# A two-block transformer kernel: score products over all 128 rows, two pools of banks for the gates, the input scaled inside its transposing product

## The chip, the core and the metric

One NeuronCore of a Trainium2 chip runs the whole program in one launch. The metric is device time in microseconds (us). TensorE (PE) has two rows in the profile: PE are the matrix products, PEld the loads of the stationary operand, which can run beside a product. VectorE is DVE, ScalarE is ACT, GpSimd is POOL, and SP issues DMA transfers. L163 is line 163 of the kernel before.

## The reference, cut to what matters

`x` is [1, 512, 1024] in float32, and everything is float32. The first block mixes tokens by a banded attention and an RWKV-7 recurrence, merges the two under gates and ends in a feed-forward net. The second block has two layers: mLSTM beside forgetting attention, then a state-space mixer beside pooling, each followed by a convolved gated feed-forward net. The parts that the change touches:

```python
# first block: 8 heads of 64, scores scaled by 1/8, relative bias
h = rms_norm(x, pre_mix_g); proj = h @ w_in
logits = einsum(q, k) * HEAD_A**-0.5 + rel_bias ; p = softmax(logits) ; y_a = p @ v
y_b = rwkv7_time_mix(...)      # has the bonus (r * r_k * k').sum(-1) * v
merged = gate_a * (y_a @ proj_a) + gate_b * (y_b @ proj_b)
# second block, layer 0: 8 heads of 64, causal, with forget gates
logits = einsum('bhqd,bhkd->bhqk', qb, k) * scale + fq[..., :, None] - F[..., None, :]
```

## The kernel before, in words

The dense products dominate. Each float32 operand is split into a high and a low part of the tensor engine's reduced format, and a product is the sum of three (high-high, low-high, high-low). `dense_A` (L144 to L173, products on L163) gives feature tiles of W^T x for 512 tokens, two banks of PSUM a call; `dense_B` (L259, products on L281) gives token tiles. Weight chunks come by SP's queue into a ring of two and are split by ACT (L132) and DVE (L133).

Everything is unrolled. The framework's scheduler fixes each engine's order of instructions at build time: it goes by program order, takes what its own cost estimate finds ready, and so fills gaps of the attention and of the recurrences with dense products. At run time each engine takes its list strictly in that order and waits on semaphores. `order(a, b)` (L222) gives the scheduler an order of issue between two instructions and no data dependence.

The places that matter here:

- **Start** (`block1_in`, L466 to L507). For each of four token tiles ACT sums the squares of x (L491), DVE scales (L375), POOL takes the power -1/2 (L376), DVE multiplies the tile [128, 1024] by the result in place (L496), and PE transposes eight blocks of it into eight banks (L498). ACT and DVE then split the banks into xT (L502, L503), and the first dense product may begin. POOL's list has, behind the four powers, the transfers of `par` and `cst` (L495), the clear of a zero tile (L556), three clears of the state tiles S (L1440) and four transfers of zeros (L559), which have an `order` edge from L554 on DVE.
- **RWKV operands** (`rwkv_half`, twice, each for f = 0 and 1). DVE makes k' in the tile `ta` (L1323, L1324), POOL multiplies `ta` into the tile KB (L1325), DVE overwrites `ta` with the bonus operand (L1327), and PE sums it over heads (L1329).
- **Attention** (`attention_heads`, called by `attention1`, L1519, and by `layer0`, L801; twice four heads each time). A unit is one head and one of four query tiles t. PE makes the scores (L1569) of 128 queries and 128(t+1) keys; in layer 0 a bfloat16 product (L1571) adds the causal mask to the same bank. DVE adds the bias and takes the minimum of the negated row (L1573), ACT takes the exponential (L1575), PE transposes (L1583), ACT and DVE in turn copy (L1586, L1588), PE multiplies with v (L1597). Two heads share a tile of q and of k, one in rows 0 to 63 and one in rows 64 to 127, and the score product takes those 64 rows alone:

```python
hs = slice((h % 2) * 64, (h % 2) * 64 + 64)
nc.tensor.matmul(ps[:, 0:n], q[hs, t * 128 : t * 128 + 128], k[hs, 0:n], ...)
```

- **mLSTM** (`mlstm`, L944) has score products of the same kind over all 128 rows (L965). In `layer0` the four query tiles of the mLSTM and the query tiles of the attention come from one ring of four buffers (tag "q").
- **Gates** (`gate_mul`, L597). Each call is a `dense_A` of two banks from the pool `mm`, which has two; DVE multiplies each bank into the gate (L600), which frees it. There are four calls with `proj_a` and four with `proj_b`. The pools `ax` and `ax2` (two banks each) serve the RWKV half through `axt` (L1233), in turn. Behind the last call a new pool of eight banks opens for the product with `w_out`.

Of the kernel before, what the change touches and what calls it, by code (L numbers as in the profile page):

```python
# [26 lines left out]
# ---- per-feature vectors, features on partitions: name -> number of 128-columns  # L27
# [61 lines left out]
class Halves:  # L89
    """a tile [128, 2, 8, 256] (token half, feature tile, token) as [128 features, 512 tokens] of one feature tile"""  # L90
# [12 lines left out]
class Builder:  # L103
# [18 lines left out]
    # ---------------------------------------------------------------- weights  # L122
    def wchunk(self, src, a, b, keep=None):
        """a weight chunk of up to 1024 columns, split; keep: (pool, bufs) to hold it in"""
# [19 lines left out]
    def dense_A(self, xk, w, col0, pp, tag="mm", nf=2, half=None, ps=None, chunks=None, low=None):  # L144
        """nf feature tiles of W^T x, features on partitions; xk: [(hi, lo)] of [128, 512].
        half: only these 256 tokens (0 before 1, into the same banks); low: only the products with the weights'
        high (False, first) or low (True) parts"""
# [27 lines left out]
    def ahead(self, specs, pool):  # L175
        """the weights of begin, their low parts still to be made: (raw, hi, lo), the first two chunks
        in the ring of all weights; specs: (A or B, w, col0, columns)"""
# [18 lines left out]
    def ahead_hook(self, specs):  # L196
        """loads the next phase's first weights, when called"""
        def hook():
            self.nx_es.append(ExitStack())
            self.nx = self.ahead(specs, self.pool(self.nx_es[-1], "early", side="right"))  # L200
        return hook
# [22 lines left out]
    def begin(self, xk, specs):  # L224
        """the first products of a phase, the first half of the tokens before the last two tiles are there, from the
        weights loaded ahead; specs as there"""
# [32 lines left out]
    def dense_B(self, xk, w, col0, pp, tag="mm", width=512, toks=(0, 1, 2, 3), ps=None, chunks=None, low=None):  # L259
        """x W[:, col0:col0+width], tokens on partitions: {token tile: [128, width] PSUM view}; low: as in dense_A"""  # L260
# [26 lines left out]
    def close_B(self, xk, w, pp, add, post, T, pool, rest=None, lag=1, hook=None):  # L287
        """x W in two halves of the columns, the second token by token, so that what follows a token starts early;
        T: the transposes of a token, lag tokens late, the last ones in the next phase;
        rest: the tiles still to be added to the first half of the columns"""  # L290
# [16 lines left out]
    def mix_part(self, xk, w, pp):  # L307
        """column half 0: xN = ALPHA * xN + the part of the mixer's output that is ready"""
# [6 lines left out]
    def split(self, src, hi, lo, lo_eng=None):  # L315
        """hi + lo == src exactly; both of the tensor engine's reduced format"""
        nc = self.nc
        nc.scalar.activation(hi, src, AF.Copy)  # L318
        return (lo_eng or nc.vector).tensor_tensor(lo, src, hi.bitcast(F32), op=ALU.subtract)  # L319
# [17 lines left out]
    def to_T(self, xn, n, pair, t, pp, tag, k0=0):  # L337
        """xn: [128 tokens, n*128] -> columns t of pair's tiles k0..k0+n, split"""
# [20 lines left out]
    # ------------------------------------------------------------ row vectors  # L359
# [12 lines left out]
    def rsqrt(self, out, src, n, scale, eps):  # L372
        """out = (scale * src + eps) ** -0.5 on [128, n] columns"""
# [21 lines left out]
    def ln_apply(self, x, st, g, b):  # L395
        """layer norm over 1024 features in place, eps 1e-5; st: bn_stats of the halves"""
# [19 lines left out]
    # ------------------------------------------------------------------ setup  # L416
# [48 lines left out]
    # ---------------------------------------------------------- block 1 mixer  # L465
    def block1_in(self, pool):  # L466
# [3 lines left out]
        with ExitStack() as es:  # L470
# [13 lines left out]
            # the tensor engine's clock rises only while it works  # L484
# [4 lines left out]
            for t in range(4):  # L489
                r = self.stat(1)  # L490
                nc.scalar.activation(junk, xs[t], AF.Square, accum_out=r)  # L491
                i = self.rsqrt(r, r, 1, 1.0 / D, 1e-6)
# [3 lines left out]
                nc.vector.tensor_scalar(xs[t], xs[t], r, None, op0=ALU.mult)  # L496
                for k in range(8):
                    nc.tensor.transpose(ps[k][:, t * 128 : t * 128 + 128], xs[t][:, k * 128 : k * 128 + 128], self.ident)  # L498
# [10 lines left out]
    def block1_mix(self, es, stop, early_es, ch):  # L509
# [46 lines left out]
        nc.gpsimd.memset(z, 0.0)  # L556
# [40 lines left out]
    def gate_mul(self, y, w, fp, gts):  # L597
        ps = self.dense_A(self.klist(y), self.A[w], fp * 256, self.mm)
# [118 lines left out]
    # ------------------------------------------------- second block: shared  # L717
    def close_ln(self, xk, w, gn, bn, np_, pp, last=False, rest=None, hook=None):
        """xN = LN(xN + x w), then xT or the output; rest: xN's second half is still to be multiplied by ALPHA"""
# [73 lines left out]
    def log1pexp_neg_abs(self, out, u):  # L793
        """out = ln(1 + exp(-|u|))"""
# [5 lines left out]
    # ---------------------------------------------------------------- layer 0  # L800
    def layer0(self):  # L801
# [3 lines left out]
        with ExitStack() as es:  # L805
            with ExitStack() as es2:
# [9 lines left out]
                # the first two heads' v, and gates: forget rows 0:4 (mLSTM), 32:36 and 64:68 (attention), input rows 96:100  # L816
# [19 lines left out]
                # mLSTM inputs  # L836
# [38 lines left out]
                # columns by token: c (0:4 of each 64), exp(-m) (32:36)  # L875
# [35 lines left out]
                bf = self.brow(lp, "b_fv", 512)  # L911
                for hf in range(2):
                    fq = featT(2056, "q", hf, 0.125, lambda f: bq[:, 4 + f : 5 + f])
# [5 lines left out]
                    for t in range(4):  # L919
# [3 lines left out]
                        (fq[hh // 2], fk[hh // 2], hh, lambda j, hh=hh, fv=fv: fv[:, j, hh * 64 : hh * 64 + 64], os_[hh // 2],  # L923
# [12 lines left out]
    def rows_to_T(self, o, hi, lo):  # L936
        """o: [128 tokens, 4 token tiles, 128 features] -> [128 features, 512 tokens], split"""
# [6 lines left out]
    def mlstm(self, lp, q, k, mv, og, M, sel, col, y):  # L944
        """the matrix memory, quadratic form; returns the last head's transposes"""
# [734 lines left out]
```

## Time and profile before

| what | value |
|---|---|
| three timed runs | 2109.14, 2109.42 (median), 2111.05 us |
| profiled execution, its span | 2106.5 us |
| timed median less that span | 2.9 us |
| PE busy | 2065.2 us, 98% of the span |
| DVE, ACT, POOL busy | 53%, 36%, 8% |
| chain that ended last | PE 53%, every other engine and DMA 1% or less |

The page gives the profiled execution by its span; the 2.9 us are what lies around the span, with the scatter of the runs in it. To read the profile: PE is busy nearly all the time, so a microsecond is won or lost where PE's own work gets longer or shorter or where PE waits. Spacing, from the start of one product to the start of the next, is what a product costs in a stream; the duration of one overlaps the next one's.

### The profile page before, as it was taken

What the parts mean: (1) busy time and instruction counts of PE and PEld (TensorE: products, weight loads), DVE (VectorE), ACT (ScalarE), POOL (GpSimd) and SP (SyncE); (2) the same over time, 40 slices, a digit from 0 to 9 for tenths busy, and PEclk for the clock granted to TensorE, in tenths of its full rate; (3) what the DMA queues carried; (4) which work ended last, traced back from release to release, by engine and by line L of the source; (5) the groups of instructions that cost most, each with busy time, mean ns of one, the idle gap of its engine ahead of it and who ended that gap; (6) DMA issues with size and microseconds to landing.
All of it is one profiled execution on the core that took longest, in us unless ns stands there. A gap on an engine that the chain in (4) does not pass through costs nothing.

```text
span 2106.5 us, 27707 instructions
## 1 busy us (share of the span) xinstructions
PE 2065.2 (98%) x11216; PEld 1696.1 (81%) x11216; DVE 1114.8 (53%) x1831; ACT 765.6 (36%) x1213; POOL 163.5 (8%) x258
## 2 busy tenths in 40 slices
PE   8999999999999999999999999999999999999998
PEld 6678677777888888888777888888897789888886
DVE  4554455565532424544534765435576676543565
ACT  4431552144333423333333344314334534432441
POOL 1101110110000000112200000000020310000000
PEclk9999999999999999999999999999999999999999
DMA  6241125143233334232212322333322033332332
GB/s 205 71 88 42 31 71 107 42 145 104 77 94 100 93 97 125 76 107 80 61 60 91 101 89 91 100 106 109 112 74 80 31 110 101 100 100 90 100 100 91
DMA packets 175120, 192.52 MB, mean 91 GB/s; under 512 B 31560, under 2 KB 144712, under 8 KB 174992
## 3 DMA queue, kind: packets, MB, share of 16 engines
q1 hardware_dynamic: 169920, 173.40, 27.4%
q0 software_dynamic: 5072, 17.35, 2.6%
q8 instruction: 88, 1.44, 0.3%
q14 instruction: 40, 0.33, 0.1%
HBM read 184.94 MB, written 5.78 MB: 91 GB/s over the span
## 4 chain that ended last, share of the span: by engine, by line
PE 53%; DVE 1%; DMA 1%; POOL 1%; ACT 0%; issue 0%; DVEq 0%; ACTq 0%; POOLq 0%
PE psA L163 29%; PE psB L281 19%; PE pss L1569 1%; PE pso L1597 1%; PE pho L1137 1%; DMA raw<-od_w_out 1%; PE psT L345 0%; PE pspt L1583 0%; PE ppg L1176 0%; PE pss L1571 0%; PE pqk L965 0%; PE pho L973 0%; DVE wlo L133 0%; PE psr L941 0%; ACT whi L132 0%
## 5 line engine op out<-in xcount | busy, mean ns | idle before, releaser
L133 DVE TENSOR_TENSOR wlo<-raw,whi 128x1024 fp32r<-128x1024 f32 (+1 forms) x295 | 360.3, 1224 | 506.9 <-ACT whi L132 303.3
L132 ACT ACTIVATE whi<-raw 128x1024 fp32r<-128x1024 f32 (+1 forms) x295 | 311.7, 1056 | 635.7 <-PE psA L163 288.4
L163 PE MATMUL psA<-xTh,whi 128*128 128x512 f32 (+1 forms) x1616 | 416.9, 378 | 3.6 <-ACT xTh L318 1.7
L163 PE MATMUL psA<-xTl,whi 128*128 128x512 f32 (+1 forms) x1616 | 415.8, 377 | 1.3 <-DVE st L375 1.3
L163 PE MATMUL psA<-xTh,wlo 128*128 128x512 f32 (+1 forms) x1616 | 412.1, 376 | 0.0
L163 PEld LDWEIGHTS psA<-xTh,whi 128*128 128x128 f32 x1616 | 288.8, 189 | 59.6 <-issue 3.0
L163 PEld LDWEIGHTS psA<-xTl,whi 128*128 128x128 f32 x1616 | 291.1, 190 | 56.2 <-issue 2.7
L163 PEld LDWEIGHTS psA<-xTh,wlo 128*128 128x128 f32 x1616 | 286.9, 188 | 53.3 <-issue 2.3
L772 DVE SCALAR_TENSOR_TENSOR v<-psA,par,v 128x511 f32<-128x511 f32 (+1 forms) x176 | 131.3, 747 | 78.9 <-ACT v L770 76.5
L376 POOL TENSOR_TENSOR st<-st,mhalf 128x1 f32<-128x1 f32 (+1 forms) x40 | 32.9, 822 | 1266.7 <-DVE st L375 1266.5
L281 PE MATMUL psB<-whi,hidh 128*128 128x512 f32 x480 | 126.7, 390 | 0.0
L281 PE MATMUL psB<-wlo,hidh 128*128 128x512 f32 x480 | 126.4, 389 | 0.0
L281 PE MATMUL psB<-whi,hidl 128*128 128x512 f32 x480 | 126.4, 389 | 0.0
L281 PEld LDWEIGHTS psB<-whi,hidl 128*128 128x128 f32 x480 | 90.1, 188 | 18.8
L281 PEld LDWEIGHTS psB<-wlo,hidh 128*128 128x128 f32 x480 | 90.1, 188 | 18.7
L281 PEld LDWEIGHTS psB<-whi,hidh 128*128 128x128 f32 x480 | 90.0, 188 | 18.7
L770 ACT ACTIVATE v<-psA,par 128x512 f32<-128x512 f32 x88 | 67.8, 771 | 98.0 <-PE psA L163 98.0
L281 PE MATMUL psB<-whi,xTh 128*128 128x256 f32 (+2 forms) x320 | 53.4, 289 | 0.0
L281 PE MATMUL psB<-whi,xTl 128*128 128x256 f32 (+2 forms) x320 | 52.6, 287 | 0.6 <-DVE xTl L319 0.6
L318 ACT ACTIVATE xTh<-psT 128x512 fp32r<-128x512 f32 x40 | 21.9, 595 | 84.2 <-PE psT L345 84.2
L281 PE MATMUL psB<-wlo,xTh 128*128 128x256 f32 (+2 forms) x320 | 49.3, 286 | 0.0
L1575 ACT ACTIVATE sb<-sb,sm 128x128 f32<-128x128 f32 (+1 forms) x64 | 35.7, 559 | 34.1 <-DVE sm L1573 33.5
(406 smaller groups left out, 2503.2 us busy)
## 6 DMA issues: line engine op xcount, KB each, us to landing
raw<-fup SPq DMA_DIRECT2D x88, 512.0 KB, 3.5
raw<-fdn SPq DMA_DIRECT2D x44, 512.0 KB, 3.3
raw<-w_in SPq DMA_DIRECT2D x42, 512.0 KB, 3.8
raw<-w_up SPq DMA_DIRECT2D x32, 512.0 KB, 3.8
raw<-w_down SPq DMA_DIRECT2D x32, 512.0 KB, 3.7
raw<-ev_w_in SPq DMA_DIRECT2D x26, 512.0 KB, 3.7
raw<-od_w_in SPq DMA_DIRECT2D x14, 512.0 KB, 3.8
raw<-w_out SPq DMA_DIRECT2D x8, 512.0 KB, 3.7
```

The lines of the kernel that those rows point to most:

```text
L132: i = nc.scalar.activation(hi, raw, AF.Copy)
L133: self.w_ins = (i, nc.vector.tensor_tensor(lo, raw, hi.bitcast(F32), op=ALU.subtract))
L163: i = nc.tensor.matmul(o.rearrange("p (h t) -> p h t", h=2) if len(x.shape) == 3 else o, wt[:, k, fs], x, start=first and half != 1, stop= ...
L281: nc.tensor.matmul(ps[t], xk[k0 + k][a][:, t * 128 : t * 128 + 128], wt[:, k, :], start=first, stop=(end and k == kn - 1 and wt is lo), sk ...
L318: nc.scalar.activation(hi, src, AF.Copy)
L376: return nc.gpsimd.tensor_tensor(out, out, self.mhalf[:, 0:n], op=ALU.pow)
L770: nc.scalar.activation(v, ps[f], AF.Identity, scale=self.p(f"fcw{l}", 88 + ft), bias=self.p(f"fcb{l}", ft))
L772: nc.vector.scalar_tensor_tensor(v[:, sh:], ps[f][:, : 512 - sh], self.p(f"fcw{l}", tap * 44 + ft), v[:, sh:], op0=ALU.mult, op1=ALU.add)
L1137: nc.tensor.matmul(po[:, t, :], w[:, (t - j) * 128 : (t - j) * 128 + 128], xdt[j][:, h * 64 : h * 64 + 64], start=(j == 0 and t == 0), sto ...
L1569: nc.tensor.matmul(ps[:, 0:n], q[hs, t * 128 : t * 128 + 128], k[hs, 0:n], start=True, stop=cmask is None, skip_group_check=True)
L1575: nc.scalar.activation(sb[:, 0:n], sb[:, 0:n], AF.Exp, scale=-1.0, bias=sm[:, t : t + 1], accum_out=sm[:, 4 + t : 5 + t])
L1597: nc.tensor.matmul(po[:, t, :], pT[:, j * 128 : j * 128 + 128], v(j), start=(t == 0 and j == 0), stop=(j == t), skip_group_check=True)
```

## The change

- x is no longer multiplied in place. DVE makes a 128x128 diagonal tile from the identity and the factor, and the product that transposes multiplies by it (a float32 product in place of a transpose).
- The transfers of `par` and `cst` get their `order` edge from that diagonal of the last tile; the clears of the zero tile and of S get one from `x_ready`, the last instruction of L503 on DVE.
- The bonus operand goes into the tile `kkn`, whose readers are done, in place of `ta`.
- Every second call of `gate_mul` takes its two banks from `ax` and `ax2`.
- Each head has its own tile of q, 128 rows, of which the 64 rows of the other head are cleared once by POOL; the score product takes all 128 rows of q and k. In `attention1` these are four tiles beside the ring of k, in `layer0` the four buffers of the ring "q", for both halves. ACT writes the even heads' rows, DVE the odd heads'.
- Comments are removed; they change no instruction.

```diff
 block1_in:
-                i = self.rsqrt(r, r, 1, 1.0 / D, 1e-6)
+                self.rsqrt(r, r, 1, 1.0 / D, 1e-6)
+                dg = ld.tile([128, 128], F32, name=self.nm("dg"))
+                i = nc.vector.tensor_scalar(dg, self.ident, r, None, op0=ALU.mult)
                 if t == 3:
                     for n in ("par", "cst"):
                         self.order(i, nc.gpsimd.dma_start(getattr(self, n), A[n]))
-                nc.vector.tensor_scalar(xs[t], xs[t], r, None, op0=ALU.mult)
                 for k in range(8):
-                    nc.tensor.transpose(ps[k][:, t * 128 : t * 128 + 128], xs[t][:, k * 128 : k * 128 + 128], self.ident)
+                    nc.tensor.matmul(ps[k][:, t * 128 : t * 128 + 128], xs[t][:, k * 128 : k * 128 + 128], dg, start=True, stop=True)
 block1_mix:
-        nc.gpsimd.memset(z, 0.0)
+        self.order(self.x_ready, nc.gpsimd.memset(z, 0.0))
 gate_mul:
-        ps = self.dense_A(self.klist(y), self.A[w], fp * 256, self.mm)
+        ps = [self.axt(1, self.nm("psA")) for _ in range(2)] if fp % 2 else None
+        ps = self.dense_A(self.klist(y), self.A[w], fp * 256, self.mm, ps=ps)
 layer0:
+                fq = self.head_tiles(lp, 4, tag="q", bufs=4)
                 for hf in range(2):
-                    fq = featT(2056, "q", hf, 0.125, lambda f: bq[:, 4 + f : 5 + f])
+                    ps = self.dense_A(xk, W, 2056 + hf * 256, mm)
+                    for f in range(2):
+                        b = bq[:, 4 + 2 * hf + f : 5 + 2 * hf + f]
+                        nc.scalar.activation(fq[2 * f][0:64, :], ps[f][0:64, :], AF.Identity, scale=0.125, bias=b[0:64, :])
+                        nc.vector.tensor_scalar(fq[2 * f + 1][64:128, :], ps[f][64:128, :], 0.125, b[64:128, :], op0=ALU.mult, op1=ALU.add)
...
-                        (fq[hh // 2], fk[hh // 2], hh, lambda j, hh=hh, fv=fv: ...
+                        (fq[hh], fk[hh // 2], hh, lambda j, hh=hh, fv=fv: ...
 rwkv_half:
-            nc.vector.scalar_tensor_tensor(ta, r, self.p("r_k", ft), ta, op0=ALU.mult, op1=ALU.mult)
+            nc.vector.scalar_tensor_tensor(kkn, r, self.p("r_k", ft), ta, op0=ALU.mult, op1=ALU.mult)
...
-            nc.tensor.matmul(psb, self.c("bones", 128), ta, start=True, stop=True)
+            nc.tensor.matmul(psb, self.c("bones", 128), kkn, start=True, stop=True)
...
-            nc.gpsimd.memset(s, 0.0)
+            self.order(self.x_ready, nc.gpsimd.memset(s, 0.0))
 attention1:
+        qz = self.head_tiles(ap, 4)
         for hf in range(2):
...
+            ps = self.dense_A(xk, w_in, hf * 256, mm)
+            for f in range(2):
+                nc.scalar.activation(qz[2 * f][0:64, :], ps[f][0:64, :], AF.Copy, scale=0.125)
+                nc.vector.tensor_scalar(qz[2 * f + 1][64:128, :], ps[f][64:128, :], 0.125, None, op0=ALU.mult)
...
+    def head_tiles(self, pool, n, **kw):
+        out = [pool.tile([128, 512], F32, name=self.nm("qz"), **kw) for _ in range(n)]
+        for h, t in enumerate(out):
+            self.nc.gpsimd.memset(t[64:128, :] if h % 2 == 0 else t[0:64, :], 0.0)
+        return out
 attention_heads:
-            nc.tensor.matmul(ps[:, 0:n], q[hs, t * 128 : t * 128 + 128], k[hs, 0:n], start=True, stop=cmask is None, skip_group_check=True)
+            nc.tensor.matmul(ps[:, 0:n], q[:, t * 128 : t * 128 + 128], k[:, 0:n], start=True, stop=cmask is None, skip_group_check=True)
```

## Rows read from the trace of the kernel before

**Rows 1.** The page's first part: busy time, share of the span and instructions of each engine.

```profile
PE 2065.2 (98%) x11216; PEld 1696.1 (81%) x11216; DVE 1114.8 (53%) x1831; ACT 765.6 (36%) x1213; POOL 163.5 (8%) x258
```

**Rows 2.** The waits of PE: who waited for whom, then us in total, times, longest us.

```profile
PE psb L1329 <- DVE ta L1327: 5.7, 3, 2.2
PE psT L498 <- DVE x L496: 3.9, 2, 2.9
PE psr L941 <- POOL ho L1004: 2.3, 3, 1.3
```

**Rows 3.** PE's timeline in the attention of the first block (start, us, instruction, rows*columns of the array, shape; x2 because a float32 product is two instructions).

```profile
133.05 0.40 PE L163 MATMUL psA<-xTl,whi 128*128 128x512 f32 x1
133.38 1.12 PE L1569 MATMUL pss<-qk,qk 64*128 64x512 f32 x2
134.43 0.55 PE L1583 MATMUL pspt<-start,sb 128*128 128x128 f32 x3
134.82 0.56 PE L1597 MATMUL pso<-v,pT 128*128 128x64 f32 x4
...
135.81 0.49 PE L1569 MATMUL pss<-qk,qk 64*128 64x128 f32 x2
136.23 0.88 PE L1597 MATMUL pso<-v,pT 128*128 128x64 f32 x6
```

**Rows 4.** The chain that ended last, two pieces (start, us, what): undisturbed streams of L163 and of transposes.

```profile
1080.88 15.66 PE psA L163 x69
...
1177.83 0.87 PE psT L345 x8
```

**Rows 5.** PE's timeline in the mLSTM of layer 0, where score products take all 128 rows.

```profile
993.61 1.02 PE L965 MATMUL pqk<-q,k 128*128 128x512 f32 x2
994.47 0.39 PE L973 MATMUL pho<-mv,w 128*128 128x129 f32 x2
...
998.42 0.39 PE L965 MATMUL pqk<-q,k 128*128 128x128 f32 x2
998.64 0.61 PE L973 MATMUL pho<-mv,w 128*128 128x129 f32 x4
```

**Rows 6.** PE's timeline in the attention of layer 0.

```profile
1113.67 0.50 PE L1583 MATMUL pspt<-start,sb 128*128 128x128 f32 x3
1114.10 0.48 PE L1569 MATMUL pss<-k,q 64*128 64x128 f32 x2
1114.51 0.23 PE L1571 MATMUL pss<-cm,idb 128*128 128x128 bf16 x1
1114.55 0.60 PE L281 MATMUL psB<-whi,y2h 128*128 128x256 f32 x3
```

**Rows 7.** Busy time by stretch: part of the first block's attention, part of layer 0's, and the first dense products (PEclk is the granted share of TensorE's clock).

```profile
121.00:140.00 19.00, 19.00 (x99) 12.50 (x99) 14.76 (x57) 8.43 (x26) 1.40 (x4) 1.00 0.18 56
1046.00:1078.00 32.00, 32.00 (x185) 21.84 (x186) 15.58 (x50) 14.46 (x43) 2.24 (x4) 1.00 0.17 48
16.60:20.00 3.40, 3.34 (x9) 2.63 (x10) 3.40 (x6) 3.40 (x6) 0.00 (x0) 0.57 0.99 357
```

**Rows 8.** The timeline of all engines at the first bonus (in brackets the idle time before and what ended it).

```profile
78.23 0.69 DVE L1324 SCALAR_TENSOR_TENSOR ta<-ta,rkv 128x512 f32<-128x512 f32 x1
...
79.06 2.12 POOL L1325 TENSOR_TENSOR KB<-ta,eLm 128x512 f32<-128x512 f32 x1 [4.07 <-DVE ta L1324]
...
81.21 0.75 DVE L1327 SCALAR_TENSOR_TENSOR ta<-rkv,par,ta 128x512 f32<-128x512 f32 x1 [1.16 <-POOL KB L1325]
82.02 1.13 PE L1329 MATMUL psb<-ta,cst 128*128 128x512 f32 x2 [1.78 <-DVE ta L1327]
```

**Rows 9.** PE's timeline where a product waited for a gate's bank.

```profile
433.38 1.21 PE L163 MATMUL psA<-yah,whi 128*128 128x512 f32 x4 [1.52 <-DVE gate L600]
...
442.24 1.17 PE L163 MATMUL psA<-yah,whi 128*128 128x512 f32 x4 [0.36 <-DVE gate L600]
...
481.69 2.14 PE L281 MATMUL psB<-whi,mgh 128*128 128x512 f32 x8 [0.78 <-DVE gate L600]
```

**Rows 10.** The timeline of all engines at the start: the last two token tiles of x; the last row is the instruction from which the four transfers of L559 have their order edge.

```profile
9.70 0.19 ACT L491 ACTIVATION_READ_ACCUMULATOR junk<-x 128x1 f32 x1
9.92 0.75 DVE L496 TENSOR_SCALAR x<-x,st 128x1024 f32<-128x1024 f32 x1 [0.66 <-POOL st L376]
...
10.59 0.15 DVE L375 TENSOR_SCALAR st<-st 128x1 f32<-128x1 f32 x1
...
11.31 0.60 POOL L495 DMA_DIRECT2D par<-par  x1
11.40 3.31 DVE L496 TENSOR_SCALAR x<-x,st 128x1024 f32<-128x1024 f32 x1 [0.66 <-POOL st L376]
...
12.43 0.98 POOL L556 MEMSET zero<- 128x1024 f32 x1
...
14.08 0.74 POOL L559 DMA_DIRECT2D tD<-zero  x1
...
14.77 1.09 PE L498 MATMUL psT<-start,x 128*128 128x128 f32 x8 [2.95 <-DVE x L496]
...
37.78 0.43 DVE L554 TENSOR_SCALAR lw<-sh 128x512 f32<-128x512 f32 x1 [0.70 <-ACT sh L553]
```

More of the change, by code (lines that the diff above doesn't have):

```diff
@@ L922, in layer0 @@
                     self.attention_heads(lb, [
-                        (fq[hh // 2], fk[hh // 2], hh, lambda j, hh=hh, fv=fv: fv[:, j, hh * 64 : hh * 64 + 64], os_[hh // 2],
+                        (fq[hh], fk[hh // 2], hh, lambda j, hh=hh, fv=fv: fv[:, j, hh * 64 : hh * 64 + 64], os_[hh // 2],
                          lambda hh=hh: fbias(4 * hf + hh), (idb, cm)) for hh in range(4)])
@@ L1529, in rbias @@
             return lambda t: b[:, 384 - 128 * t : 512]
+        qz = self.head_tiles(ap, 4)
         for hf in range(2):
-            qk = []
-            for base, sc in ((0, 0.125), (512, 1.0)):
-                ps = self.dense_A(xk, w_in, base + hf * 256, mm)
-                row = []
-                for f in range(2):
-                    t = ap.tile([128, 512], F32, tag=f"qk{base}", bufs=2, name=self.nm("qk"))
-                    nc.scalar.activation(t, ps[f], AF.Copy, scale=sc)
-                    row.append(t)
-                qk.append(row)
+            ps = self.dense_A(xk, w_in, hf * 256, mm)
+            for f in range(2):
+                nc.scalar.activation(qz[2 * f][0:64, :], ps[f][0:64, :], AF.Copy, scale=0.125)
+                nc.vector.tensor_scalar(qz[2 * f + 1][64:128, :], ps[f][64:128, :], 0.125, None, op0=ALU.mult)
+            ps = self.dense_A(xk, w_in, 512 + hf * 256, mm)
+            kt = []
+            for f in range(2):
+                t = ap.tile([128, 512], F32, tag="k", bufs=2, name=self.nm("k"))
+                nc.scalar.activation(t, ps[f], AF.Copy)
+                kt.append(t)
             v = ap.tile([128, 4, 256], F32, tag="v", bufs=1, name=self.nm("v"))
@@ L1546, in attention1 @@
             self.attention_heads(ap, [
-                (qk[0][hh // 2], qk[1][hh // 2], hh, lambda j, hh=hh, v=v: v[:, j, hh * 64 : hh * 64 + 64], o[hh // 2],
+                (qz[hh], kt[hh // 2], hh, lambda j, hh=hh, v=v: v[:, j, hh * 64 : hh * 64 + 64], o[hh // 2],
                  lambda hh=hh: rbias(4 * hf + hh), None) for hh in range(4)])
@@ L1565, in scores @@
             sm, po, bf = st[id(hd)]
-            hs = slice((h % 2) * 64, (h % 2) * 64 + 64)
             n = 128 * (t + 1)
             ps = at.tile([128, 512], F32, tag="ax", name=self.nm("pss"))
-            nc.tensor.matmul(ps[:, 0:n], q[hs, t * 128 : t * 128 + 128], k[hs, 0:n], start=True, stop=cmask is None, skip_group_check=True)
+            nc.tensor.matmul(ps[:, 0:n], q[:, t * 128 : t * 128 + 128], k[:, 0:n], start=True, stop=cmask is None, skip_group_check=True)
             if cmask is not None:
```

## The prediction, made before the change was run

> **What bounds the kernel now.** I read the busy times first: PE works 98% of the span, DVE about half, the others less [rows 1]. So a term counts only if it shortens PE's own stream or removes one of PE's waits. The waits of PE come next: the longest is the bonus product on its operand, then the transposes of x on the scaled x, then the mLSTM's transposes on a gate made by POOL [rows 2]. These are a few us out of 2106. The third view is PE's timeline, read by spacing: how long it is from one product's start to the next one's. There the score products stand out, though PE never looks idle in them.
>
> **Scores.** A product of 512 columns over 64 rows holds PE from 133.38 to 134.43, 1.05 us. The L163 ahead of it holds PE 0.33 [rows 3], where a free stream has 15.66 / 69 = 0.227 a product; the three transposes behind it take 0.39, where a free stream has 3 x 0.109 = 0.33 [rows 4]. So PE also loses 0.10 ahead and 0.06 behind. The mLSTM makes the same shape, in the same type, over 128 rows: 0.86, and 0.22 at 128 columns [rows 5], against 0.42 over 64 rows [rows 3]. The extra inside is thus 0.19 to 0.20, whatever the length; I take 0.19 for the two lengths between. A full-height product needs no other rows than these show, and the zeros cost nothing on PE.
> First block: 32 products x (0.19 + 0.10 + 0.06) = 11.2 us. Layer 0: ahead of a score three transposes take 0.43 instead of 0.33, and a product of 128 columns 0.41 instead of 0.22; the mask product behind it takes 0.04, so I count nothing there [rows 6]: 32 x 0.29 = 9.3. Together 20.5.
> Not all of it stays. Eight units of the first block fall into 121 to 140, where DVE also makes the triangular inverse: it is busy 14.8 of 19.0 us, ACT 8.4, PE all of it [rows 7]. Eight products free 2.8 us, DVE has 4.2 idle, but not where the scores want it; my estimate is that half returns as waits, 1.4. In layer 0 DVE is busy 15.6 of 32, and nothing returns. Net **19.1**. Bounds: 20.5 above; below, if only the losses ahead and behind go, 32 x 0.16 + 32 x 0.10 = 8.3.
>
> By the Trainium skill, page "TensorE: Matmul & The Clock Gate", section "Why this matters for your kernels", a product with few rows takes the same time as one with 128, and the gain of slicing at row 64 is that products in distinct row groups run side by side. By that rule the 0.19 stays, the scores give 8.3 and the kernel 2094, which is a rival below. The rows speak against both halves: the same shape differs by 0.19, and no two products here lie side by side, since neighbours are separated by transposes and belong to the same head.
>
> **Bonus.** DVE has k' at 78.92, but waits 1.16 for POOL, which reads `ta` for 2.12 us; PE then waits 1.78 for the operand [rows 8]. In the whole kernel that wait is 5.7 us in three places [rows 2]. With `kkn` as the target the operand needs no POOL. DVE may still stand behind a weight split of its list. Three times 1.16 is 3.5, and the scheduler, which knows of the freedom, can place the product better; at most 5.7 goes. I take **4.2**, bounds 2.5 and 5.7. The next in line are the transposes of KB, which still need POOL's product; POOL may be slower with DVE beside it, and that is the lower bound.
>
> **Gates.** Products wait 1.52, 0.36 and 0.78 for L600 [rows 9]. The first two are a call that wants the banks of the call before; in turn with `ax` it wants those of two calls before, which L600 has had 5 us for. The third is the first product with `w_out`, whose bank belonged to the last gate; the last gate is now in `ax`, and the first of the eight new banks are those of `mm`. **2.7**, bounds 1.9 (the first two) and 2.7.
>
> **Start.** DVE's scaling of the last tile takes 3.31 us where the tile before took 0.75: it begins 0.09 behind POOL's transfers and ends when POOL's burst of transfers and clears has ended, at about 14.1 [rows 10]. Are the clears really later? The four transfers of L559 have an order edge from L554, which runs at 37.78, and still start at 14.08 [rows 10]. So an order edge between two engines holds nothing at run time, and since POOL has no other work to put in between, the burst follows the last power as before. What does move: L375 of the last tile stood behind the scaling of the tile before until 10.59, though ACT's sum was there at 9.89; the diagonal is an eighth of the work, so the power and the burst come 0.7 earlier, and behind the burst DVE needs 0.1 instead of some 0.6. That is 1.1 earlier; the first bank's product is then float32, 0.22 [rows 5] instead of 0.109 [rows 4], and ACT's splits, longer than either, set the rest. **1.0**. Bounds: -0.5 if all eight products of the last tile (8 x 0.11 = 0.9 longer) stood on the path; above, if the edge does hold, 2.8 more (the burst from 11.31 to 14.08). Further, the first dense products ran at a granted clock of 0.57 [rows 7], between its levels of 1.2 and 2.4 GHz, after PE had stood 2.95 us and made eight transposes. Seven products at twice their 0.227 cost some 1.4; if the shorter gap spares it, 1.4 more. Upper bound 5.2, of which I count 4.4.
>
> **Clears.** POOL makes eight clears of 64x512. The zero tile of 128x1024 took 0.98 [rows 10], so about 0.5 each, 2 us in either attention. In the first block they come long before the first score. In layer 0 they need the mLSTM's last reads of the ring, so they fall among POOL's work for the mLSTM, on which PE waits 2.3 already [rows 2]: **0.5 lost**, bounds 0 and 2.5. Behind a clear on POOL's queue stand the gates of the last heads; their transposes wait for those. The four extra DVE copies of q in each attention are covered by the next projection, 48 products of 0.227, before which no bank is wanted back.
>
> **Sum.** 19.1 + 4.2 + 2.7 + 1.0 - 0.5 = 26.5. On the profiled span of 2106.5 that is 2080.0; the timed median lies 2.9 higher, so 2109.4 - 26.5 = **2083**.
>
> **Rivals.**
> 1. *The softmax chain takes over.* With PE faster, a unit waits for DVE and ACT instead, and half of the 20.5 returns. For it: a unit's chain is serial, and 121 to 140 has DVE at 78%. Against it: layer 0 has half of DVE free [rows 7], and dense products fill in between. 19.1 becomes 10.2: 2092.
> 2. *Only the losses around the scores go*, the extra inside having another cause than the height. Against it: rows 5 beside rows 3. Scores 8.3: 2094.
> 3. *Slower: the clock falls in the attention.* At the start the clock was below its upper level after a gap of about 3 us [rows 7, 10]; in the attention it is 1.00 and PE without a gap. If the chain of rival 1 left gaps of that size in a unit, PE would run at the lower level, and a us of PE's work costs another. One half of one attention is 32 us [rows 7]: 2083 + 32 = 2115. It decides once some 30 us of PE's work run at the lower level; a unit lasts 2 us, so a gap would have to be longer than a unit.
> 4. *The ring "q" holds the second half back.* Its q tiles now wait for the scores of the first half, banks of `mm` stay taken, and PE lacks filler: in the worst case a whole projection, 48 x 0.227 = 10.9, 2094. Against it: that projection ends behind the last scores now (its stream runs from 1080.88 on [rows 4]).
>
> **How the numbers follow.** My forecast has 0.70, with its own range of 2075 to 2091; rivals 1, 2 and 4 have 0.12, 0.08 and 0.03, rival 3 has 0.04, and 0.03 is left for a reordering by the scheduler that eats the gain. The low end is all upper bounds: 20.5 + 5.7 + 2.7 + 4.4 = 33.3, 2076, so 2075. The high end takes in rivals 1, 2 and 4: 2096. A measurement of this kernel tells about 0.2%, 4.2 us, from no change. Faster by more: 0.70 + 0.12 + 0.08 + 0.03 = 0.93; within: 0.03; slower: 0.04.
>
> **What would show it.** Right: score products of 128 rows spaced 0.86 at 512 columns, with L163 ahead at 0.227; no wait on L600; the bonus wait below 2; the first dense product near 15.6 and the clears still beside the last diagonal. Wrong: PE waiting on L1573, L1575 or the copies for more than 5 us in all (rival 1), a spacing of 1.05 (rival 2), a granted clock below 1.00 in an attention (rival 3), PE idle before the second half of layer 0 (rival 4), and at the start a diagonal of 0.1 us right behind its power (then the edge holds).

## The result, and the profile of the changed kernel

| what | before | changed |
|---|---|---|
| timed median (lowest to highest, runs) | 2110.24 us (2109.14 to 2114.76, 4) | 2095.47 us (2092.03 to 2098.52, 4) |
| ratio, 95% interval | 1 | 0.9927 [0.9915, 0.9939] |
| span of the profiled execution | 2106.5 us | 2093.7 us |

The kernel is 14.8 us faster. The forecast had 26.5 us less (2083); the range, 2075 to 2096, just holds the result. So the question is where 12 us went.

Busy times on the page of the changed kernel; they answer [rows 1]:

```profile
PE 2053.7 (98%) x11248; PEld 1701.4 (81%) x11248; DVE 1121.9 (54%) x1839; ACT 766.0 (37%) x1213; POOL 161.6 (8%) x266
```

PE has 11.5 us less to do, and is still the bound. Its waits, beside [rows 2] (us in total, times, longest us):

```profile
PE psb L1337 <- DVE kkn L1335: 3.9, 3, 1.6
PE psr L949 <- POOL ho L1012: 3.2, 3, 1.2
PE pspt L1600 <- ACT pT L1603: 2.8, 1, 2.8
...
PE psA L163 <- DVE sh L1238: 2.4, 1, 2.4
...
PE psA L163 <- DVE qz L1544: 1.0, 1, 1.0
...
PE psA L163 <- DVE qz L921: 0.7, 1, 0.7
...
PE psB L281 <- DVE gate L603: 0.3, 1, 0.3
```

The bonus wait went from 5.7 to 3.9 only. `pspt` was 1.9 in the trace of before, `sh` 0.5, `psr` 2.3; all three grew. The two waits for `qz`, the new copies of q on DVE, are new. The waits for the gates (L600 before, L603 now) are all but gone.

Now PE's timeline in the first block's attention, the place of [rows 3]:

```profile
133.47 0.40 PE L163 MATMUL psA<-xTl,whi 128*128 128x512 f32 x1
133.71 1.04 PE L1586 MATMUL pss<-k,qz 128*128 128x512 f32 x2
134.58 0.49 PE L1600 MATMUL pspt<-start,sb 128*128 128x128 f32 x3
134.91 0.56 PE L1614 MATMUL pso<-v,pT 128*128 128x64 f32 x4
```

The score product holds PE 0.87 (134.58 - 133.71) where it held 1.05; the L163 ahead holds it 0.24 instead of 0.33, the transposes behind 0.33 instead of 0.39. That is the forecast (0.86, 0.227, 0.33) to about 0.01 us. Summed over all products of a line, from each start to the next one's: the 128 score instructions took 46.6 us and take 34.2, the transposes behind (L1583, L1600) 20.2 and 17.7, the products with v (L1597, L1614) 35.2 and 32.8.

To see where the time goes I lined up the two traces product by product: the start of the same product in each, and how far ahead the changed kernel is. The table gives the change of that lead stage by stage (us; minus is gained; stages end at the time given, in the trace of before). The other columns are experiments told below: the changed kernel profiled once more (e12), the changed kernel with scores over 64 rows (e1), and two versions that go further (e6, e10).

| stage, to | changed | e12 | e1 | e6 | e10 |
|---|---|---|---|---|---|
| start, 41.4 | +2.8 | +2.3 | +0.1 | -2.6 | -2.4 |
| RWKV operands, 118.8 | -0.5 | -0.5 | -0.5 | +0.2 | +0.2 |
| attention of the first block, 283.5 | -6.7 | -6.8 | 0.0 | -6.5 | -6.4 |
| second RWKV half, 385.8 | -0.3 | -0.5 | -0.5 | -0.5 | -0.5 |
| gates, 506.5 | -3.0 | -3.0 | -3.0 | -3.0 | -3.0 |
| to the mLSTM, 985.4 | -1.9 | -1.7 | +0.3 | +0.6 | +0.6 |
| mLSTM of layer 0, 1035.6 | +2.2 | +2.2 | +2.1 | +1.1 | 0.0 |
| attention of layer 0, 1171.4 | -7.8 | -8.6 | 0.0 | -8.7 | -8.6 |
| the rest | +2.5 | +0.8 | +2.8 | +0.6 | -1.5 |
| sum | -12.7 | -15.8 | +1.3 | -18.8 | -21.6 |

In the last row but one, and in the one before the mLSTM, no instruction was changed. What differs there is mainly TensorE's clock; near the end PE also waits for a weight split (L132), 1.25 in the trace of e1 and 0.51 in that of e12. The changed kernel by stretches (columns as in [rows 7]; the last three are the granted clock, the DMA share and GB/s):

```profile
37.80:41.20 3.40, 3.40 (x10) 2.62 (x9) 1.62 (x3) 1.21 (x2) 0.14 (x1) 0.50 0.41 136
239.20:242.60 3.40, 3.40 (x10) 2.72 (x9) 2.48 (x7) 0.00 (x0) 2.57 (x2) 0.50 0.00 0
1563.50:1566.90 3.40, 3.40 (x10) 2.61 (x9) 2.75 (x4) 2.84 (x4) 0.00 (x0) 0.51 0.02 5
1621.60:1628.40 6.80, 5.78 (x15) 3.71 (x16) 4.12 (x14) 2.70 (x8) 3.08 (x5) 0.50 0.01 4
1648.90:1652.30 3.40, 3.19 (x4) 1.51 (x5) 2.37 (x11) 1.78 (x5) 0.04 (x1) 0.50 0.02 5
...
121.00:140.00 19.00, 18.90 (x117) 14.97 (x116) 15.38 (x60) 10.30 (x29) 1.40 (x4) 1.00 0.32 68
```

The first five are stretches at 0.50, the lower level of 1.2 GHz; one of 3.4 us costs about 1.6 where PE is busy, since the products in it are spaced 0.43 instead of 0.227. Before had them at 16.1, 531.5 (6.8 us), 1637.4 and 1661.3. The one at 239.2 stands in the middle of an attention, where the clock had been 1.00. In the last row DVE and ACT are busier than in [rows 7], and PE still works 18.90 of 19.

### The profile page after: what moved, and what is told of

Read it like the earlier page. It is cut to its first block, busy times and chain, and to the rows that moved or that the text cites. A ratio compares the mean times of both kernels' runs of the same rounds, so it can differ in the third digit from the quotient of the medians.

```text
span 2093.7 us, 27791 instructions
## 1 busy us (share of the span) xinstructions
PE 2053.7 (98%) x11248; PEld 1701.4 (81%) x11248; DVE 1121.9 (54%) x1839; ACT 766.0 (37%) x1213; POOL 161.6 (8%) x266
## 4 chain that ended last, share of the span: by engine, by line
PE 49%; DVE 1%; DMA 0%; ACT 0%; issue 0%; POOL 0%; DVEq 0%; ACTq 0%; POOLq 0%
PE psA L163 28%; PE psB L281 17%; PE pss L1586 1%; PE pso L1614 1%; PE pho L1145 1%; PE psT L345 1%; DMA raw<-ev_w_out 0%; PE pspt L1600 0%; PE ppg L1184 0%; ACT whi L132 0%; DVE wlo L133 0%; PE pcb L1118 0%; DVE pa L1174 0%; DVE xbc L1084 0%; PE pc L1065 0%
## 5 line engine op out<-in xcount | busy, mean ns | idle before, releaser
L132 ACT ACTIVATE whi<-raw 128x1024 fp32r<-128x1024 f32 (+1 forms) x295 | 311.5, 1056 | 635.4 <-PE psA L163 286.1
L163 PE MATMUL psA<-xTh,whi 128*128 128x512 f32 (+1 forms) x1616 | 417.9, 378 | 6.4 <-DVE sh L1238 2.4
L163 PE MATMUL psA<-xTl,whi 128*128 128x512 f32 (+1 forms) x1616 | 417.5, 378 | 1.3 <-DVE st L375 1.3
L163 PE MATMUL psA<-xTh,wlo 128*128 128x512 f32 (+1 forms) x1616 | 412.4, 376 | 1.1 <-DVE wlo L133 0.6
L163 PEld LDWEIGHTS psA<-xTh,whi 128*128 128x128 f32 x1616 | 288.1, 189 | 64.5 <-issue 3.7
L163 PEld LDWEIGHTS psA<-xTl,whi 128*128 128x128 f32 x1616 | 291.2, 190 | 55.6 <-DVE st L375 1.6
L163 PEld LDWEIGHTS psA<-xTh,wlo 128*128 128x128 f32 x1616 | 287.5, 188 | 55.1 <-issue 1.8
L281 PEld LDWEIGHTS psB<-whi,hidl 128*128 128x128 f32 x480 | 90.1, 188 | 18.8
L1586 PE MATMUL pss<-k,qz 128*128 128x128 f32 (+3 forms) x128 | 45.9, 444 | 0.0
```

What stands on the lines that cost most here:

```text
L132: i = nc.scalar.activation(hi, raw, AF.Copy)
L163: i = nc.tensor.matmul(o.rearrange("p (h t) -> p h t", h=2) if len(x.shape) == 3 else o, wt[:, k, fs], x, start=first and half != 1, stop= ...
L281: nc.tensor.matmul(ps[t], xk[k0 + k][a][:, t * 128 : t * 128 + 128], wt[:, k, :], start=first, stop=(end and k == kn - 1 and wt is lo), sk ...
L1586: nc.tensor.matmul(ps[:, 0:n], q[:, t * 128 : t * 128 + 128], k[:, 0:n], start=True, stop=cmask is None, skip_group_check=True)
```

## The experiments

All times are medians, beside runs of the kernel before on the same chip; ratios are to those.

**e1: the height alone.** The instruction lists of all engines are those of the changed kernel; only the rows of the score product differ.

```diff
-            nc.tensor.matmul(ps[:, 0:n], q[:, t * 128 : t * 128 + 128], k[:, 0:n], ...
+            nc.tensor.matmul(ps[:, 0:n], q[h % 2 * 64 :, :][0:64, t * 128 : t * 128 + 128], k[h % 2 * 64 :, :][0:64, 0:n], ...
```

> The changed kernel, but the score product takes the 64 rows of its own head again; order of instructions, copies and clears stay. Theory (the scores were sized about right, the missing gain was lost elsewhere): the height alone is worth what the trace gave in the two attentions, 6.7 + 8.5 = 15.2 us, so 2110.5 us, with a spacing of 1.05 at 512 columns. Rival 1 (the softmax chain takes half of it back): 10 us, 2105.5. Rival 2 (only the losses around the scores): the spacing stays 0.87 and the time is about 2104.

Measured: 2110.2 us (2108.0 to 2111.5, 11 runs), ratio 0.9994 [0.9985, 1.0002]. The spacing is 1.06 again:

```profile
132.64 0.40 PE L163 MATMUL psA<-xTl,whi 128*128 128x512 f32 x1
132.96 1.12 PE L1586 MATMUL pss<-k,qz 64*128 64x512 f32 x2
134.02 0.55 PE L1600 MATMUL pspt<-start,sb 128*128 128x128 f32 x3
```

The height is worth 14.7 us (2110.2 - 2095.5), as the theory had it; the rivals miss by about 5 and 6 us, and the lowest of the eleven runs is 2108.0. It follows that all the rest of the change together is worth nothing that these runs can tell (0.9994; at most 3.2 us by the interval), where the forecast had 7.4: bonus 4.2, gates 2.7, start 1.0, clears -0.5.

**e2 and e3: the start alone.** e2 is the changed kernel with the three start edits taken back, e3 the kernel before with only them (the hunks of `block1_in`, of the zero tile and of S in the diff above).

> The changed kernel with the start of before (x scaled in place, transposed; clears without the order edge). Theory (the new start reaches the first weights earlier, the weights come later, and a wait with a stretch of low clock follows): the start is worth -3.5 us of gain, so about 2092.0, and the wait of 2.4 us at 34 us is 0.5. Rival (the new start is worth the 1.0 that was forecast and the loss in the trace was chance): 2096.5.

> The kernel before with only the new start. Theory: slower by 2.8, the difference that stood at 41 us in the two traces: 2113.0. Rival (forecast): 2109.2.

Measured: e2 2094.4 us (2092.3 to 2094.8), ratio 0.9918 [0.9903, 0.9932]; e3 2110.7 (2109.0 to 2114.7), ratio 1.000 [0.999, 1.001]. Both lie between the two expectations: the start is worth nothing, perhaps a us of loss. The theory took the loss of 2.8 in one trace for the rule. At 41.4 us the new start stands at +2.8 and +2.3 in the two traces of the changed kernel, but at +0.1 and +0.6 in those of e1 and e3, and at +0.5 to +0.8 in those of e4, e5 and e7, which had no low clock there; the old start of e2 stands at +0.7 itself.

**e4: all copies of q on ACT.** In both attentions, for example:

```diff
-                nc.vector.tensor_scalar(qz[2 * f + 1][64:128, :], ps[f][64:128, :], 0.125, None, op0=ALU.mult)
+                nc.scalar.activation(qz[2 * f + 1][64:128, :], ps[f][64:128, :], AF.Copy, scale=0.125)
```

> The changed kernel with all copies of q on ACT, none on DVE. Theory (a copy on DVE stands behind DVE's list and holds a bank, PE waited 0.99 and 0.73 for it): 1.7 less, 2093.8. Rival (ACT is then late with weight splits and gives it back): 2095.5 or more.

Measured: 2091.3 us (2086.6 to 2095.8, 6 runs), ratio 0.9908 [0.9893, 0.9924]: 4.2 less by the medians, more than the 1.7 of the theory, with ranges that overlap. Both waits for `qz` are gone. By the stages the mLSTM's loss falls from 2.2 to 1.1, so one of the two copies cost 1.1. In the first block nothing is left of the gain at 118.8 us, and from 41.4 to 283.5 this kernel gains 6.2 where the changed one gains 7.2; new waits stand there, 0.8 for `VW`, 0.6 for `bon` and 1.1 in the attention. So the stages tell of some 0.1 of the 4.2. The mean granted clock was 0.995 in its six runs and 0.993 in ten of the changed kernel (e12 has six of them); by the price of a stretch above I estimate some 3 us from that.

**e5: the bonus in `ta` again.**

```diff
-            nc.vector.scalar_tensor_tensor(kkn, r, self.p("r_k", ft), ta, op0=ALU.mult, op1=ALU.mult)
+            nc.vector.scalar_tensor_tensor(ta, r, self.p("r_k", ft), ta, op0=ALU.mult, op1=ALU.mult)
```

> The changed kernel with the bonus operand in `ta` again. Theory (DVE's own list, with a weight split in it, makes the operand late, and POOL's read comes on top by little): slower by about 1, 2096.5, the waits for the bonus 5 us in all instead of 3.9. Rival (forecast: POOL's read was the cause): slower by 4.2, 2099.7.

Measured: 2091.9 us (2090.6 to 2099.0, 5 runs), ratio 0.9923 [0.9909, 0.9937]; that is no slower than the changed kernel, where both expectations had it slower. The wait for the bonus is 5.3 in all. A worth of 4.2 (2099.7, a ratio near 0.995) is outside the interval; the 1.4 us by which the waits differ is inside it. In its one trace, that of its slowest run, stretches of low clock stand behind two of these waits (from 97.6 behind one of 2.17, from 312.6 behind one of 1.93); the changed kernel, with waits of 1.25 and 1.65 there, has none, but neither has before, with 2.17 and 1.76. So what the wait costs with its clock is not settled by these runs.

**e6: zeros, par and cst really later**, on the kernel of e4.

```diff
+            for n in ("par", "cst"):
+                nc.sync.dma_start(getattr(self, n), A[n])
             junk = ld.tile([128, 1024], F32, name="junk")
...
-                if t == 3:
-                    for n in ("par", "cst"):
-                        self.order(i, nc.gpsimd.dma_start(getattr(self, n), A[n]))
...
-        self.order(self.x_ready, nc.gpsimd.memset(z, 0.0))
+        for j in range(2):
+            nc.gpsimd.tensor_scalar(z[:, j * 512 : j * 512 + 512], lw[1], 0.0, None, op0=ALU.mult)
```

> The kernel with all copies of q on ACT (2091.3), and in it the burst of POOL taken out of the start by data, not by an order edge: the zero tile is made from lw, which exists at about 40 us, and par and cst go by SP behind the first weights. Theory (the burst holds the last diagonal, and its transfers hold the next weights): the last diagonal takes about 0.3, the first dense product comes near 13.5 us instead of 15.9, and the wait at 34 us is below 0.5; 3 us less, 2088.3. Rival (the weights' own transfers set this stretch): nothing is left of it at 51 us, 2091.3.

Measured: 2089.0 us (2087.6 to 2090.0), ratio 0.9898 [0.9883, 0.9914]. The interval, 2085.4 to 2091.9, holds both expectations; the trace tells them apart. The lead at 41.4 us is 2.6 and the same at 51 us, and the wait for `sh` is no longer among those of PE:

```profile
10.54 0.81 POOL L1448 MEMSET S<- 128x256 f32 x3
10.63 0.81 DVE L497 TENSOR_SCALAR dg<-start,st 128x128 f32<-128x128 f32 x1 [0.66 <-POOL st L376]
13.38 2.42 ACT L503 ACTIVATE xTh<-psT,start 128x512 fp32r<-128x512 f32 x4 [2.23 <-PE psT L499]
...
28.19 1.06 ACT L132 ACTIVATE whi<-raw 128x1024 fp32r<-128x1024 f32 x1 [2.65 <-DMA raw<-w_in]
```

The first dense product starts at 14.91, not at 13.5: the diagonal is there at 11.44, and ACT then waits until 13.38 for PE, whose transposing products of 0.23 were not through.

**e7 and e8: the clears of layer 0 behind POOL's last product of the mLSTM** (e7 on the kernel of e4, e8 on that of e6).

```diff
-                fq = self.head_tiles(lp, 4, tag="q", bufs=4)
+                fq = self.head_tiles(lp, 4, behind=self.last_ho, tag="q", bufs=4)   # an order edge to each clear
```

> The kernel with all copies of q on ACT (2091.3), and in it the clears of layer 0 get an order edge behind POOL's last product of the mLSTM. Theory (a clear at the head of POOL's list waits for PE's last read of its tile, and a power of the mLSTM stands behind it): the step of about 1.1 between 1000 and 1035 us goes, 2090.2. Rival (the step comes from something else in the new order): 2091.3.

> Both edits together on the kernel with all copies of q on ACT. Theory: 4.1 us less than 2091.3, 2087.2. Rival: if neither edit is worth anything, 2091.3.

Measured: e7 2098.9 us (2096.6 to 2100.5), ratio 0.9946 [0.9934, 0.9959]; e8 2097.2 (2090.2 to 2097.3), ratio 0.993 [0.9917, 0.9942]. e7 is slower than e4 by 7.6 and e8 than e6 by 8.2, against theory and rival. The step before 1010 us did go, but the edge made the scheduler order the mLSTM's end anew:

```profile
1015.12 1.16 PE L949 MATMUL psr<-start,ho 128*128 128x128 f32 x3 [1.27 <-POOL ho L1012]
...
1017.34 0.33 PE L949 MATMUL psr<-start,ho 128*128 128x128 f32 x1 [1.06 <-POOL ho L1012]
...
1017.44 0.61 PE L163 MATMUL psA<-xTh,whi 128*128 128x512 f32 x1
```

The last head's transposes now come before their data, with no dense product in between; PE waits 2.3, and a stretch of low clock follows from 1017.6. In both traces the mLSTM loses 5.0 where e4 and e6 lose 1.1; that is 3.9 of the 8. The rest shows as low clock elsewhere: the trace of e7 has four stretches more than that of e4 besides this one (from 522.7, 918.6, 1625.2 and 1649.1), and the slower runs of e8, at 2097, had a mean clock of 0.990, the profiled one, at 2090, had 0.996. Why they are more in these two stays open.

**e9, e10 and e11.** e9 is e6 with x scaled in place and transposed as before. e10 is e6 with each clear of layer 0 behind POOL's last product of its own head (`behind=self.ho`, one entry a head). e11 is both.

> The kernel of e6 (2089.0), in which x is again scaled in place and transposed; zeros, par and cst stay late. Theory (with the burst gone PE itself sets the start, 32 products at 0.23 against transposes at 0.109): the first dense product comes about 1 us before the 14.9 of e6, and the total is 2088.0 to 2089.0, as the weights set what follows. Rival (PE's gaps between the transposes bring back the stretch of low clock at 16 us): 1.4 more, 2090.4.

> The kernel of e6 (2089.0), in which each clear of layer 0 has an order edge behind POOL's last product of its own head. Theory (the clear waited at the head of POOL's list): the step of 1.1 us in the mLSTM goes and nothing is bunched, 2087.9. Rival (as in e7, another order of PE's list costs more than the step): 2092.

> Both edits of e9 and e10 together. Theory: 2086.9 to 2087.9. Rival: 2092 or more, if either rival holds.

Measured: e9 2089.3 us (2084.1 to 2089.6), ratio 0.9886 [0.9871, 0.9902]; e10 2088.1 (2083.9 to 2090.2), 0.9884 [0.9868, 0.990]; e11 2089.5 (2087.1 to 2091.9), 0.9893 [0.9879, 0.9908]. In e9 the first dense product starts at 14.43, half a us before that of e6, and nothing of it shows in the median; the stretch of the rival is not in its trace, though in that of e11 (from 14.8). In e10 the mLSTM's loss is 0.0 where e6 has 1.1, and PE waits there as before the change:

```profile
PE psr L949 <- POOL ho L1013: 2.3, 3, 1.3
```

e10 has the lowest median, 24 us or 1.16% below before on that chip; e6, e9 and e11 are within its interval, so that only the step in the mLSTM tells e10 from e6. e9 comes within 0.3 of its theory's total, with half of the 1 us at the first product; e11 lies between its two expectations.

**e12: the changed kernel again.**

> The changed kernel again, as it was. If its four runs (2092.0 to 2098.5) are a fair sample: 2095.5. If stretches of low clock fell badly in them: 2092 to 2093, and with them the worth of all parts is 2 to 3 us more than the first result says. In the trace a wait of 2.8 us at about 236 us, with a stretch of low clock behind it.

Measured: 2095.65 us (2092.3 to 2100.1, 6 runs), ratio 0.9926 [0.991, 0.9941]. The first result stands; it was not bad luck. The wait of 2.8 is at its place, with a stretch of low clock from 238.6.

## Why the prediction was right, and which of its terms were not

The direction was right, and so was the main mechanism, the height of the scores. That the range held is luck: 2095.5 lies above the forecast's own range of 2075 to 2091, and it is below 2096 only because the rivals 1, 2 and 4 were taken in, none of which came. Two of the signs went against the forecast: the bonus wait is 3.9 where it was to be below 2, and an attention has a granted clock of 0.50.

| term | forecast | measured | from |
|---|---|---|---|
| scores | 19.1 | 14.7 | e1 against changed |
| bonus | 4.2 | about 1 | e5: waits 5.3 against 3.9; median no slower |
| gates | 2.7 | 3.0 | stages, in all columns |
| start | 1.0 | 0 to -1 | e2, e3 |
| clears | -0.5 | -1.1 | stages, e10 against e6 |
| copies of q | 0 | -1.1 | the one in layer 0: stages, e6 against changed |

These come to some 16 against the 14.8 of the medians; the 1 between is less than the runs can tell.

**Scores.** The mechanism and the size of each product were right: the spacing 0.87, and in e1 1.06 with the same lists; all score products together hold PE 12.4 less (46.6 - 34.2), where 64 times 0.19 is 12.2. By the Trainium skill, page "TensorE: Matmul & The Clock Gate", section "Why this matters for your kernels", a product over few rows takes as long as one over 128; for these float32 products e1 shows 0.19 us more at 512 columns, and the measurement decides. The rivals 1 and 2 would have given nearly the measured time, and for the wrong reason; without e1 the time would have spoken for them. What failed first is the term "given back, 1.4", and its place. It was put into 121 to 140, where DVE is busiest; there PE lost 0.1 (18.90 of 19). It came at 236, where ACT has another task than softmax (changed kernel, all engines):

```profile
233.84 1.28 ACT L1517 ACT_TABLE_LOAD   x1
...
235.14 0.69 ACT L1517 ACTIVATE gsq<-psv,d_c 128x512 f32<-128x512 f32 x1
...
235.29 0.92 PE L163 MATMUL psA<-xTh,wlo 128*128 128x512 f32 x2
235.84 1.28 ACT L1519 ACT_TABLE_LOAD   x1
237.14 1.15 ACT L1519 ACTIVATE gsq<-gsq 128x512 f32<-128x512 f32 x2
...
238.19 0.49 ACT L1592 ACTIVATE sb<-sb,sm 128x256 f32<-128x256 f32 x1
...
238.68 0.25 ACT L1603 ACTIVATE pT<-pspt 128x128 f32<-128x128 f32 x1
...
238.99 0.56 PE L1600 MATMUL pspt<-start,sb 128*128 128x128 f32 x2 [2.78 <-ACT pT L1603]
```

Between two units of the attention ACT takes the group norm of the RWKV half, with two table loads. From the first table load to the end of the copy `pT` the chain is as long as before, 5.09 (233.84 to 238.93; 238.14 to 243.23 in the kernel before); PE comes to it 0.9 earlier and waits 2.78 instead of 1.90. The product that waited, in the kernel before:

```profile
243.28 0.44 PE L1583 MATMUL pspt<-start,sb 128*128 128x128 f32 x2 [1.90 <-ACT pT L1586]
```

Then comes the stretch of low clock, 1.6 us. This is rival 3 in small. Its condition, a gap longer than a unit of 2 us, was met once, and 3.4 us of PE's work ran at the lower level, not some 30. Of the eleven traces with full-height scores ten have a stretch here (all but e5), of the three others (before, e1, e3) none. The length of the wait alone does not decide it: e5 has the same 2.78 and no stretch, while the seven traces with all copies of q on ACT and a stretch here have two waits, of 1.0 and 2.0 with about 3 us between them. So 2.5 was given back (0.9 of wait, 1.6 of clock) where the forecast had 1.4. The other size that failed is that of the losses around the scores. In e12 the two attentions give 17.0 once the stretch is left out (6.8 + 1.6 + 8.6), so 17.9 with the wait; less the 12.4 inside that is 5.5, where 32 x 0.16 and 32 x 0.10 made 8.3. Product by product between e1 and e12, whose lists are the same, the products ahead of a score lose 5.7, nearly the 6.4 forecast, but those behind 1.2 instead of 1.9: I had sized these by a few neighbours. The other 1.4 comes back in small pieces, 0.4 of it as waits at 137.7 and 145.4. Together 1.1 + 2.8 of the 4.4; the last 0.5 is less than the medians tell.

**Bonus.** The step that failed is "DVE waits for POOL" as the cause of PE's wait. The second place, in the changed kernel; it answers [rows 8]:

```profile
94.27 1.22 DVE L133 TENSOR_TENSOR wlo<-raw,whi 128x1024 fp32r<-128x1024 f32 x1
...
95.40 0.69 DVE L1332 SCALAR_TENSOR_TENSOR ta<-ta,rkv 128x512 f32<-128x512 f32 x1
...
96.13 0.75 DVE L1335 SCALAR_TENSOR_TENSOR kkn<-rkv,par,ta 128x512 f32<-128x512 f32 x1
96.24 1.76 POOL L1333 TENSOR_TENSOR KB<-ta,eLm 128x512 f32<-128x512 f32 x1 [3.71 <-DVE ta L1332]
...
97.03 0.67 PE L1337 MATMUL psb<-kkn,cst 128*128 128x512 f32 x1 [1.25 <-DVE kkn L1335]
```

DVE no longer waits for POOL, and PE still waits 1.25 where it waited 2.17: a weight split of 1.22 stands ahead of L1332. So POOL's read was only the last link of a chain. The scheduler did use its freedom, but to place the product earlier: PE runs two dense products of the group ahead of it where before and e5 run four. At the first place the operand itself got slower:

```profile
82.59 2.13 POOL L1333 TENSOR_TENSOR KB<-ta,eLm 128x512 f32<-128x512 f32 x1 [4.79 <-DVE ta L1332]
...
83.50 1.77 DVE L1335 SCALAR_TENSOR_TENSOR kkn<-rkv,par,ta 128x512 f32<-128x512 f32 x1
```

Beside POOL's product it takes 1.77 instead of 0.75 and ends 0.55 behind it (85.27 and 84.72), nearly as late as in e5, where it waits and ends 0.78 behind it. The forecast had feared a slower POOL; that came at the second place, where POOL began second (1.76, and 1.26 in before). At the third no split stands ahead; the product comes 13 dense products earlier in PE's list than before, and PE waits 1.65 where it waited 1.76. Against e5 the three waits are shorter by 0.24, 0.92 and 0.28. The lower bound of 2.5 was too high as well, since a wait of DVE was taken for a wait of PE.

**Gates.** Right; only the wait of 0.3 at `w_out` is left where [rows 9] has 0.78.

**Start.** That the order edges hold nothing back was right; [rows 10] come back nearly as they were, with the next wait added:

```profile
10.88 0.60 POOL L498 DMA_DIRECT2D par<-par  x1
10.96 2.85 DVE L495 TENSOR_SCALAR dg<-start,st 128x128 f32<-128x128 f32 x1 [0.66 <-POOL st L376]
...
12.00 0.98 POOL L558 MEMSET zero<- 128x1024 f32 x1
...
12.89 0.84 POOL L1448 MEMSET S<- 128x256 f32 x3
...
13.65 0.55 POOL L561 DMA_DIRECT2D tD<-zero  x1
...
13.86 2.05 PE L500 MATMUL psT<-dg,x 128*128 128x128 f32 x16 [0.65 <-DVE dg L495]
...
15.91 0.50 PE L163 MATMUL psA<-xTh,whi 128*128 128x512 f32 x1
...
33.25 1.06 ACT L132 ACTIVATE whi<-raw 128x1024 fp32r<-128x1024 f32 x1 [3.51 <-DMA raw<-w_in]
...
35.48 0.74 DVE L1238 SCALAR_TENSOR_TENSOR sh<-psA,par,sh 128x511 f32<-128x511 f32 x1
...
36.28 0.50 PE L163 MATMUL psA<-xTh,whi 128*128 128x512 f32 x1 [2.36 <-DVE sh L1238]
```

The last diagonal takes 2.85, until POOL's clears have ended (12.89 + 0.84); the three before it took 0.29 each. By the Trainium skill, page "SBUF — State Buffer", section "SBUF: two separate sides", DVE in some modes and POOL hold one pair of ports by turns, and the one that comes second stands still; the trace agrees here (2.85, and 0.81 beside the three clears of S in e6), and shows DVE standing still over several of POOL's instructions in a row. The burst comes 0.43 earlier (11.31 to 10.88), where 0.7 was forecast, and the first dense product 0.75 (16.66 to 15.91), where 1.0 was; and the low clock at 16 is gone, as the upper bound had it. What was left out is what is late next: the weights. ACT's split of the fifth chunk waits for its transfer until 33.25, where before it was 32.08; PE, which comes earlier, then waits 2.36 for `sh` instead of 0.49, and the low clock comes here. In e6, with POOL's four transfers of 512 KB of zeros out of the way, that split starts at 28.19, and the start is 2.6 ahead: the burst's transfers held the weights back. The zeros are 2 MB of that; e6 also moves `par` and `cst`, 0.7 MB, and no run tells the two apart. Why the same transfers brought the weights a us later than before stays open.

**Clears and copies.** The clears lost 1.1, in the way and within the bounds that the prediction gave: a clear at the head of POOL's list waits 0.98 for PE's last read of its tile, and the power that the next gates need stands behind it.

```profile
997.58 0.52 POOL L1567 MEMSET qz<- 64x512 f32 x1 [0.98 <-PE pqk L973]
...
998.18 1.02 POOL L376 TENSOR_TENSOR st<-st,mhalf 128x4 f32<-128x4 f32 x1
```

"Covered by the next projection, before which no bank is wanted back" was wrong: the copy on DVE holds a bank, and PE waits 0.99 and 0.71 for it (the second in layer 0, where one copy cost 1.1 by the stages).

```profile
81.03 0.69 DVE L1544 TENSOR_SCALAR qz<-psA 64x512 f32<-64x512 f32 x1
...
81.78 0.96 PE L163 MATMUL psA<-xTh,whi 128*128 128x512 f32 x3 [0.99 <-DVE qz L1544]
```

## What to carry to other kernels

A product that gets shorter pays in full at its own place, but the engines beside it do not move: look along the whole stretch for the one chain that PE now reaches too early, and put its price, with the clock that falls behind the wait, into the sum. A wait is worth what the next-latest input leaves of it, not its length; for each wait that a change removes, ask which row comes next. Where an edit leaves computation alone, as the rows of a product, undo just that in the same lists; it settles the size of a term to a few us, where the total can't tell two stories apart.

## What the runs showed of the hardware

The same program differs from run to run by the stretches of low clock: the changed kernel took 2092.0 to 2100.1 us in ten runs, with mean clocks of 0.996 for the fastest and 0.992 for the slowest. A difference of 0.004 is 17 us at the lower level, and at 1.6 us for 3.4 that makes 8 us, all of the difference (an estimate from these figures). Before took 2107.3 to 2117.6 in 23. They come at few places, and in the traces I read each of the early ones (16, 37, 239, 531) stands behind or within a wait of PE of 1.3 to 3 us. Whether one comes at a given place differs from run to run: after the wait for `sh` of 2.4 and 2.0 it came, after those of 1.5 to 1.7 in five traces it did not. A single trace therefore misleads by some us, as it did the theory of e2 and e3.
